# The second block's token mixers: spatial gating ahead of the context's output, a regrouped output projection, other PSUM banks, and the heads' transposes one unit later

## The chip, the cores and the metric

One core of a Trainium2 chip runs the whole program in one launch. The metric is device time in microseconds, lower is better; the profile's times are microseconds unless marked ns.

## The reference, cut to what matters

Two transformer blocks run one after the other on 512 tokens of width 1024. The change is in the second one, which has two layers and carries a context of 256 tokens beside x. In each layer the projected input is split into ten parts of 256 columns, and four mixers of 256 columns each are joined and projected:

```python
y_a = conformer_conv(a_val, a_gate, ...)      # 31-tap depthwise conv, layer norm, silu
y_b = diff_attention(q1, q2, k1, k2, v, ...)  # 4 heads, x attends to context and x; rms norm per head
y_c = spatial_gating(u, sv, ...)              # gelu, layer norm, a 128x128 token mix per chunk
y_d = short_conv_mixer(bg, cg, xin, ...)      # 3-tap depthwise conv between two gates
return concatenate([y_a, y_b, y_c, y_d], -1) @ w_out
```

Layer 0 runs these mixers for the context too (its attention sees only the context); layer 1 uses the context for keys and values alone. x then gets its gated sum and an MLP of width 4096.

## The kernel before, in words

Everything is in float32. A weight or activation that meets in a large matmul is split into a rounded part and a rest (`whalf`: `whi` on ACT at line 149, `wlo` on DVE at line 150; `split` for activations), and `mm3` makes three matmuls out of one (lines 157 to 159, `tok3` lines 164 to 166 where tokens are the stationary side). So one group of an input part is 2 halves x 4 k-tiles x 3 = 24 matmuls into one PSUM bank. Weights come by DMA into `raw` (4 buffers) and live in 3 buffers each of `whi` and `wlo`, for all stages.

The code is written with tiles and pools, and a planner makes each engine's stream from it ahead of time. It goes by program order, may bring forward what is ready, and a region under `bg()` or with a negative offset comes after work that stands later in the program. On the chip every engine runs its own stream in order. A tile waits for the tiles that had its place before; a pool takes the place of one that was closed.

The order of layer 0 of the second block, with its names: `mc` is the context's `Mixer`, `mx` that of x.

1. `mc.conv`, `mc.qkv`, `mc.spatial`, `mc.short`, then `mc.attention` in PSUM set `ps_k` (banks: g 4, mm 1, po 1, sc 2).
2. `mx.conv`, `mx.qkv` (parts 0, 1, 3, 4, 2 of x), still in `ps_k`.
3. `mc.conv_norm` (mean, square sums, rsqrt, silu of the convolution, lines 992 to 1013), then `mc.out_part("cdab")`: 8 output groups of 8 k-tiles, which write the context's sum back by DMA.
4. `mx.spatial`: part 6 by tokens, gelu and layer norm into `sv`; part 5, gelu; then 24 token-mix matmuls with `sv` into `ps.mm()` (lines 941 to 946), read by DVE at line 951.
5. `mx.attention` in set `ps_d` (g 3, mm 1, po 1, and three banks in one tile `sc3`). 16 units of one head and 128 queries: scores (line 1057), row maximum (DVE, line 1061), two exponentials (ACT, line 1065), the difference (DVE, line 1074), 6 transposes (line 1081), 12 matmuls with v (line 1084), which is 22 instructions of PE. `weights` of the next unit goes ahead of `apply` of this one. Each pair of heads ends in `heads_norm`, which scales the heads and transposes them (line 1106) into a y tile.
6. Work is hung into the units: at unit 1 `mx.short` (6 groups of 24 matmuls, under `bg()`), at unit 4 `mx.conv_norm`, then `out_part("cda")` under `bg()` (8 groups of 18), and one convolution tap of each half per unit while there are any left (line 872; the first 20 of 31 are given out earlier, under `bg(1000)`).
7. `out_part("b")` in set `ps_e` (8 groups of 6), each followed by the sum into x (line 1139) and its square, and the norm of x for the MLP.

Layer 1 has set `ps_m` (g 5, mm 3) for steps 2 and 4, the context's keys and values in step 2, and no step 1 and 3.

Of the kernel before, what the change touches and what calls it, by code (L numbers as in the profile page):

```python
# [19 lines left out]
P = 128  # L20
# [59 lines left out]
def tile_net(ctx: ExitStack, tc: tile.TileContext, wst, vec, crow, lrow, sgw, cst, xT, xN, cT, out):  # L80
# [14 lines left out]
    def close_pool(g):  # L95
        g.__exit__(None, None, None)
# [91 lines left out]
    def split(act, src, scale=None):  # L188

        if scale is None:  # L190
            A.copy(act[:, 0], src)
            V.tensor_sub(act[:, 1], src, act[:, 0].bitcast(F32))
        else:
            A.activation(act[:, 0], src, AF.Copy, scale=scale)
            V.scalar_tensor_tensor(act[:, 1], src, scale, act[:, 0].bitcast(F32), op0=ALU.mult, op1=ALU.subtract)
# [107 lines left out]
    ps = PS("ps_u", mm=8)  # L303
# [425 lines left out]
    def xsums():  # L729
        return Sums(SX, xp.tile([P, SX], F32, tag="acc", name=nm("acc")))  # L730
# [77 lines left out]
    class Mixer:  # L808
# [207 lines left out]
        def attention(self, k, bp, stp_, keys, between):  # L1016
# [9 lines left out]
            def load_head(h):  # L1026
                hd = Head()
                hd.h = h
                hd.q = stp_.tile([96, 2, s.n], F32R, tag="qst", name=nm("qst"), bufs=ST_BUFS)
                hd.k = stp_.tile([96, 2, nkeys], F32R, tag="kst", name=nm("kst"), bufs=ST_BUFS)  # L1030

                def stack(dst, src, blk, rows):
                    for i, hl in enumerate(rows):
                        nc.sync.dma_start(dst[32 * i:32 * i + 32].bitcast(F32),
                                          src[32 * blk:32 * blk + 32, hl].bitcast(F32))

                for w in range(2):
                    blk = 2 * (h % 2) + w
                    stack(hd.q[:, w], s.q[h // 2], blk, (0, 1, 0))
                    o = 0  # L1040
                    for q in keys:
                        stack(hd.k[:, w, o:o + q.n], q.k[h // 2], blk, (0, 0, 1))
                        o += q.n
                return hd
# [43 lines left out]
            def heads_norm(o, r1):  # L1088

                of = o.rearrange("p t h d -> p (t h) d")  # L1090
                rf = r1.rearrange("p t h -> p (t h)")
                sq = bp.tile([P, ng, 64], F32, tag="osq", name=nm("osq"), bufs=1)
                A.activation(sq, of, AF.Square)
                ms = const.tile([P, 16], F32, tag="ms", name=nm("ms"), bufs=3)
                m2 = const.tile([P, 16], F32, tag="ms2", name=nm("ms2"), bufs=2)
                V.tensor_reduce(ms[:, :ng], sq, axis=AX.X, op=ALU.add)
                V.tensor_mul(m2[:, :ng], rf, rf)
                V.tensor_mul(ms[:, :ng], ms[:, :ng], m2[:, :ng])
                V.tensor_scalar(ms[:, :ng], ms[:, :ng], 1.0 / 64.0, EPS, op0=ALU.mult, op1=ALU.add)
                rs = rstd_small(ms[:, :ng], ng)  # L1100
                V.tensor_mul(m2[:, :ng], rs[:, :ng], rf)
                V.tensor_mul(sq, of, m2[:, :ng].unsqueeze(2).broadcast_to([P, ng, 64]))
                pq = ps.mm()
                s2 = sq.rearrange("p (t h) d -> p t (h d)", h=2)
                for i in range(s.nt):
                    T.transpose(pq[:, i * P:(i + 1) * P], s2[:, i], ident)
                a = self.y_tile("b")
                split(a, pq[:, :s.n], k.subg)
                self.y["b", len([q for q in self.y if q[0] == "b"])] = a

            heads = {0: load_head(0)}
            units = [(h, qt) for h in range(4) for qt in range(s.nt)]
            nxt = weights(heads[0], 0)
            for un, (h, qt) in enumerate(units):
                hd = heads[h]
                if qt == 0:
                    if h < 3:
                        heads[h + 1] = load_head(h + 1)
                    if h % 2 == 0:
                        po = ps.mm("po")[:, :ng * 64].rearrange("p (t h d) -> p t h d", h=2, d=64)  # L1120
                        r1 = const.tile([P, s.nt, 2], F32, tag="r1", name=nm("r1"), bufs=2)
                    hd.r1 = r1
                    hd.po = po
                cur = nxt
                if un + 1 < len(units):
                    h2, qt2 = units[un + 1]
                    nxt = weights(heads[h2], qt2)
                apply(hd, qt, *cur)
                if un in between:
                    between[un]()  # L1130
                if self.taps[0] < 31:
                    self.conv_taps(k, self.taps[0] + CONV_STEP)
                if qt == s.nt - 1 and h % 2:
                    heads_norm(po, r1)


        def add(self, m, p, done):
# [5 lines left out]
        def out_part(self, names, done=None, bank=None):  # L1143
# [3 lines left out]
            for half in range(2):  # L1147
                w = {n: whalf((key, 2 + half), "ab".index(n), 512) for n in names if n in "ab"}
                for pair in range(2):
                    if "c" in names:  # L1150
                        w["cd"] = whalf((key, half), pair, 256)
                    for i in range(2):
# [9 lines left out]
                            mm3(p, hi[:, kk, c], lo[:, kk, c], a[:, 0], a[:, 1], e == 0, e == len(seq) - 1)  # L1162
                        self.add(4 * half + 2 * pair + i, p, done)


    g_ca, ctmp = open_pool("ctxb", side="right")
    kc = mix_consts(0, kvc, ctmp)
# [5 lines left out]
    mc.short()  # L1173
    close_pool(g_ca)
    ps.close()
    ps = PS("ps_k", g=4, mm=1, po=1, sc=2)
    g_cb, cb = open_pool("ctxb", side="right")
    mc.attention(kc, cb, cb, [sc], {})
    def load_rope(pool):
        rope = pool.tile([P, 2, SX], F32, tag="rope", name=nm("rope"))  # L1180
        nc.sync.dma_start(rope, cst[:, P + 9 * P:P + 9 * P + 1024].rearrange("p (a t) -> p a t", a=2))
# [7 lines left out]
    for l in range(2):  # L1189
# [2 lines left out]
        g_hc, hcp = open_pool("hc")  # L1192
        if l == 1:
            ps.close()
            ps = PS("ps_m", g=5, mm=3)
            kx = mix_consts(l, mix, hcp)
        else:
            kx = kc
# [7 lines left out]
            close_pool(g_c)  # L1206
        mx.qkv({"x": mix, "c": mix}, load_rope(hcp))
        close_pool(g_hc)
        if l == 0:

            mc.conv_norm(kc)
            sc.x = []
            for m in range(0, NT, 2):
                t = cmix.tile([P, 2, SC], F32R, tag="h", name=nm("xc"), bufs=8).bitcast(F32)
                nc.sync.dma_start(t, cT[:, m:m + 2])
                sc.x += [t[:, 0], t[:, 1]]
            mc.out_part("cdab", lambda m: nc.sync.dma_start(c_dram[m], sc.x[m]))
            close_pool(g_cb)
            close_pool(g_cm)
        g_st, stk = open_pool("stk")  # L1220
        g_y, yp = open_pool("yp", side="right")
        g_s, sgp = open_pool("sgp", side="right")
        mx.spatial(kx, sgp)
        close_pool(g_s)
        ps.close()
        ps = PS("ps_d", **PSD)
        g_b, bp = open_pool("mixb", side="right")
# [3 lines left out]
                mx.short()  # L1231

        def middle():
            mx.conv_norm(kx)
            with bg():
                mx.out_part("cda")

        mx.attention(kx, bp, stk, [sx, sc], {EARLY: early, MIDDLE: middle})
        close_pool(g_b)
        close_pool(g_st)  # L1240
        ps.close()
        ps = PS("ps_e", mm=8)
        sx.acc = xsums()
        mx.out_part("b", lambda m: sx.acc.add(None, sx.x[m], m, mx.tt("sq")))
        pbx = rstd_bcast(mix, sx.acc, SX, 1.0 / 1024, tile=mx.tt("rb"))
        close_pool(g_mix)
        close_pool(g_y)
        if l == 0:
            close_pool(g_kvc)

# [96 lines left out]
P_BUFS = 2  # L1347
HID_BUFS = 10
TA_BUFS = 6
CONV_TAPS = 20  # L1350
CONV_STEP = 1
CONV_BG = 1000
EARLY = 1
BIAS_BG = 200
MIDDLE = 4
ADA_HEAD = 0
PUMP = 6
L_BUFS = 8
# [146 lines left out]
```

## Time and profile before

| | us |
|---|---|
| median of 3 runs | 2176.56 (2175.21 to 2178.31) |
| the profiled execution | 2175.18 |
| its span, first to last instruction | 2173.3 |
| PE busy (matmuls) | 2053.4 |
| DVE busy | 1424.4 |
| ACT busy | 810.1 |
| layer 0, x's query projection to x's first scores | 787.3 to 860.7 |
| layer 0, x's attention, first scores to last product with v | 860.7 to 971.3 |
| layer 1, the same | 1661.6 to 1773.7 |

PE is TensorE's matmuls, PEld its weight loads, DVE VectorE, ACT ScalarE, POOL GpSimd, SP SyncE, which issues the DMAs. A busy share says how long an engine had something in hand, not that it was what the end waited for; matmuls are pipelined, so their number in a stretch says more than their busy time. A wait is told as: who waited, for whom, how long in all, how often, and the longest.

### The profile page before, as it was taken

Reading aid. Unit: us, or ns where it says so; the run is one execution under the profiler, and the core shown is the slowest. Engines: PE = TensorE matmul, PEld = TensorE weight load, DVE = VectorE, ACT = ScalarE, POOL = GpSimd, SP = SyncE. Lnnn points to the kernel's source line nnn. Section 1 sums busy time; section 2 is a strip of 40 time slices with the busy share of each in tenths; the row PEclk is TensorE's granted clock in tenths of the full one; section 3 lists DMA queues with packets and bytes.
Section 4 is the critical chain, followed back from the end, with each engine's and each line's share of the span. In section 5 each row is a group of like instructions: output and inputs, shape, how many; then the busy total and the mean of one; then the engine's idle time right before and its main releaser. Section 6 shows DMA issues by size and latency. Waiting matters only on the chain.

```text
span 2173.3 us, 28000 instructions
## 1 busy us (share of the span) xinstructions
PE 2053.4 (94%) x11020; PEld 1758.3 (81%) x11020; DVE 1424.4 (66%) x2351; ACT 810.1 (37%) x1266; POOL 27.4 (1%) x28
## 2 busy tenths in 40 slices
PE   7989999999999988998999999999998998999997
PEld 5778788778889777876888888888887787888886
DVE  8778999843458999778354645534798766443444
ACT  3565333432344533645312313123434544232331
POOL 0000000000000000000000000000000000000000
PEclk9999999999999999998999999999999998999998
DMA  8523666523335444222232454422413212333331
GB/s 314 171 92 95 197 222 204 181 94 105 109 111 168 124 121 127 78 78 79 67 127 88 138 169 150 155 67 89 135 59 107 83 59 69 97 97 97 97 97 58
DMA packets 84388, 259.47 MB, mean 119 GB/s; under 512 B 11424, under 2 KB 20256, under 8 KB 84256
## 3 DMA queue, kind: packets, MB, share of 16 engines
q1 hardware_dynamic: 84256, 257.67, 37.6%
q8 instruction: 87, 1.43, 0.3%
q14 instruction: 45, 0.37, 0.1%
HBM read 242.95 MB, written 5.24 MB: 114 GB/s over the span
## 4 chain that ended last, share of the span: by engine, by line
PE 72%; DVE 18%; DMA 3%; issue 3%; ACT 3%; POOL 1%; SPq 0%; POOLq 0%; DVEq 0%; ACTq 0%
PE mm L157 15%; PE mm L159 15%; PE mm L158 15%; PE g L157 5%; PE g L158 5%; PE g L159 5%; DVE wlo L150 3%; DVE ya L872 2%; PE po L1084 2%; DVE rawa L263 2%; DVE j L263 1%; PE sc L1057 1%; DMA rawa<-wst 1%; PE mm L1081 1%; PE mm L208 1%
## 5 line engine op out<-in xcount | busy, mean ns | idle before, releaser
L149 ACT CAST whi<-raw 128x1024 fp32r<-128x1024 f32 x312 | 326.9, 1050 | 536.7 <-PE mm L158 387.4
L150 DVE TENSOR_TENSOR wlo<-raw,whi 128x1024 fp32r<-128x1024 f32 x312 | 380.5, 1222 | 210.7 <-ACT whi L149 205.9
L157 PE MATMUL mm<-h,whi 128*128 128x512 f32 (+1 forms) x992 | 361.0, 366 | 5.7 <-ACT h L338 3.6
L158 PE MATMUL mm<-h,whi 128*128 128x512 f32 (+1 forms) x992 | 361.7, 365 | 0.9 <-DVE h L712 0.9
L159 PE MATMUL mm<-h,wlo 128*128 128x512 f32 (+1 forms) x992 | 361.1, 364 | 0.8 <-DVE wlo L150 0.8
L159 PE MATMUL mm<-hid,wlo 128*128 128x512 f32 (+1 forms) x768 | 272.6, 355 | 1.0 <-DVE wlo L150 1.0
L157 PE MATMUL mm<-hid,whi 128*128 128x512 f32 (+1 forms) x768 | 273.0, 355 | 0.0
L158 PE MATMUL mm<-hid,whi 128*128 128x512 f32 (+1 forms) x768 | 272.8, 355 | 0.0
L157 PEld LDWEIGHTS mm<-h,whi 128*128 128x128 f32 x992 | 188.8, 191 | 37.1 <-ACT h L338 4.0
L158 PEld LDWEIGHTS mm<-h,whi 128*128 128x128 f32 x992 | 188.7, 190 | 31.5 <-DVE h L712 1.9
L157 PE MATMUL g<-h,whi 128*128 128x512 f32 x512 | 205.7, 402 | 8.6 <-DVE v L508 6.0
L159 PEld LDWEIGHTS mm<-h,wlo 128*128 128x128 f32 x992 | 188.6, 190 | 31.2 <-DVE wlo L150 2.0
L158 PE MATMUL g<-h,whi 128*128 128x512 f32 x512 | 204.8, 400 | 0.0
L159 PE MATMUL g<-h,wlo 128*128 128x512 f32 x512 | 204.3, 399 | 0.3 <-DVE wlo L150 0.3
L159 PEld LDWEIGHTS mm<-hid,wlo 128*128 128x128 f32 x768 | 146.1, 190 | 21.5 <-DVE wlo L150 1.4
L157 PEld LDWEIGHTS mm<-hid,whi 128*128 128x128 f32 x768 | 146.4, 191 | 20.2
L158 PEld LDWEIGHTS mm<-hid,whi 128*128 128x128 f32 x768 | 146.3, 191 | 20.0
L1284 DVE SCALAR_TENSOR_TENSOR r<-mm,r 128x512 f32<-128x512 f32 x96 | 57.4, 599 | 114.1 <-ACT r L1283 114.0
L157 PEld LDWEIGHTS g<-h,whi 128*128 128x128 f32 x512 | 98.4, 192 | 26.9 <-issue 6.2
L159 PEld LDWEIGHTS g<-h,wlo 128*128 128x128 f32 x512 | 98.1, 192 | 19.3 <-DVE wlo L150 0.7
L158 PEld LDWEIGHTS g<-h,whi 128*128 128x128 f32 x512 | 98.3, 192 | 17.9
L872 DVE SCALAR_TENSOR_TENSOR ya<-glu,caw,ya 128x512 f32<-128x512 f32 (+1 forms) x180 | 111.6, 656 | 0.5
(309 smaller groups left out, 3462.7 us busy)
## 6 DMA issues: line engine op xcount, KB each, us to landing
raw<-wst SPq DMA_DIRECT2D x312, 512.0 KB, 3.9
rawa<-wst SPq DMA_DIRECT2D x120, 512.0 KB, 4.6
qst<-q SPq DMA_DIRECT2D x48, 64.0 KB, 2.0
kst<-k SPq DMA_DIRECT2D x48, 64.0 KB, 2.0
kst<-k SPq DMA_DIRECT2D x72, 32.0 KB, 2.1
x<-xT SPq DMA_DIRECT2D x4, 512.0 KB, 5.0
hs_d<-c SPq DMA_DIRECT2D x4, 512.0 KB, 2.6
hq<-hs_d SPq DMA_DIRECT2D x4, 512.0 KB, 5.5
```

What stands on the lines that cost most here:

```text
L149: A.copy(hi, src)
L150: V.tensor_sub(lo, src, hi.bitcast(F32))
L157: T.matmul(ps, lh, rh, start=start, stop=False)
L158: T.matmul(ps, lh, rl, start=False, stop=False)
L159: T.matmul(ps, ll, rh, start=False, stop=stop)
L208: T.matmul(pt[:, i:i + 1], a[:, i * P:(i + 1) * P], ones1, start=k == 0 and i == 0, stop=k == len(self.parts) - 1 and i == nt - 1, skip_gr ...
L263: V.tensor_tensor_reduce(o, w, row, 0.5, 0.0, ALU.mult, ALU.add, d)
L872: V.scalar_tensor_tensor(self.ya[m], x, w, self.ya[m], op0=ALU.mult, op1=ALU.add)
L1057: T.matmul(st[:, o:e], hd.q[:, w, qt * P:(qt + 1) * P], hd.k[:, w, o - w * nkeys:e - w * nkeys], start=True, stop=True, skip_group_check=True)
L1081: T.transpose(pt[:, i * P:(i + 1) * P], pw[0][:, t0 + i * P:t0 + (i + 1) * P], ident)
L1084: T.matmul(hd.po[:, qt, h % 2], pth[:, i * P:(i + 1) * P], ss.v[:, kt, h], start=i == 0 and qt == 0 and h % 2 == 0, stop=i == nk - 1 and q ...
L1284: V.scalar_tensor_tensor(r, p, 0.0, r, op0=ALU.max, op1=ALU.mult)
```

## The change

Five edits, in both layers where both have the place:

- The heads' end is cut in two. `heads_norm` scales the heads and returns `finish`, which transposes and splits them; `finish` of the first pair runs after the next unit's `apply`, that of the second pair is handed to the caller.
- x's `spatial` goes ahead of the context's `conv_norm` and `out_part`. For that the pool `yp` (x's y tiles) is opened before it and on the left side, and the context attention's pool `cb` is closed at once.
- x's output projection is grouped as c and d together, then a and b together (`out_ab`): the first three of its eight groups run their a and first b k-tiles ahead of `finish`.
- PSUM sets: `ps_k` has g 3 and mm 2 (before 4 and 1), `ps_m` g 3 and mm 2 (before 5 and 3); x's last projection stays in `ps_d`'s three g banks (before `ps_e`, eight).
- Hooks: 9 taps given out early (before 20), then 2 per unit (before 1); output c, d from unit 7; `conv_norm` at unit 11 (before 4, ahead of the output).

```diff
@@ -1100,14 +1100,19 @@
                 rs = rstd_small(ms[:, :ng], ng)
                 V.tensor_mul(m2[:, :ng], rs[:, :ng], rf)
                 V.tensor_mul(sq, of, m2[:, :ng].unsqueeze(2).broadcast_to([P, ng, 64]))
-                pq = ps.mm()
-                s2 = sq.rearrange("p (t h) d -> p t (h d)", h=2)
-                for i in range(s.nt):
-                    T.transpose(pq[:, i * P:(i + 1) * P], s2[:, i], ident)
-                a = self.y_tile("b")
-                split(a, pq[:, :s.n], k.subg)
-                self.y["b", len([q for q in self.y if q[0] == "b"])] = a
-
+
+                def finish():
+                    pq = ps.mm()
+                    s2 = sq.rearrange("p (t h) d -> p t (h d)", h=2)
+                    for i in range(s.nt):
+                        T.transpose(pq[:, i * P:(i + 1) * P], s2[:, i], ident)
+                    a = self.y_tile("b")
+                    split(a, pq[:, :s.n], k.subg)
+                    self.y["b", len([q for q in self.y if q[0] == "b"])] = a
+
+                return finish
+
+            pending = None
             heads = {0: load_head(0)}
             units = [(h, qt) for h in range(4) for qt in range(s.nt)]
             nxt = weights(heads[0], 0)
@@ -1126,12 +1131,16 @@
                     h2, qt2 = units[un + 1]
                     nxt = weights(heads[h2], qt2)
                 apply(hd, qt, *cur)
+                if pending:
+                    pending()
+                    pending = None
                 if un in between:
                     between[un]()
                 if self.taps[0] < 31:
                     self.conv_taps(k, self.taps[0] + CONV_STEP)
                 if qt == s.nt - 1 and h % 2:
-                    heads_norm(po, r1)
+                    pending = heads_norm(po, r1)
+            return pending
 
 
         def add(self, m, p, done):
@@ -1162,6 +1171,31 @@
                             mm3(p, hi[:, kk, c], lo[:, kk, c], a[:, 0], a[:, 1], e == 0, e == len(seq) - 1)
                         self.add(4 * half + 2 * pair + i, p, done)
 
+        def out_ab(self, done, finish):
+
+
+            key = f"out{self.l}"
+            ps_ = {}
+
+            def part(m, steps):
+                for e in steps:
+                    n, kk = "ab"[e // 2], e % 2
+                    (hi, lo), c, a = w[n], slice((m % 4) * P, (m % 4 + 1) * P), self.y["ab"[e // 2], kk]
+                    mm3(ps_[m], hi[:, kk, c], lo[:, kk, c], a[:, 0], a[:, 1], e == 0, e == 3)
+
+            for half in range(2):
+                w = {n: whalf((key, 2 + half), i, 512) for i, n in enumerate("ab")}
+                for m in range(4 * half, 4 * half + 4):
+                    if m == 0:
+                        for i in range(3):
+                            ps_[i] = ps.g()
+                            part(i, range(3))
+                        finish()
+                    if m > 2:
+                        ps_[m] = ps.g()
+                    part(m, range(3 if m < 3 else 0, 4))
+                    self.add(m, ps_[m], done)
+
 
     g_ca, ctmp = open_pool("ctxb", side="right")
     kc = mix_consts(0, kvc, ctmp)
@@ -1173,9 +1207,10 @@
     mc.short()
     close_pool(g_ca)
     ps.close()
-    ps = PS("ps_k", g=4, mm=1, po=1, sc=2)
+    ps = PS("ps_k", g=3, mm=2, po=1, sc=2)
     g_cb, cb = open_pool("ctxb", side="right")
-    mc.attention(kc, cb, cb, [sc], {})
+    mc.attention(kc, cb, cb, [sc], {})()
+    close_pool(g_cb)
     def load_rope(pool):
         rope = pool.tile([P, 2, SX], F32, tag="rope", name=nm("rope"))
         nc.sync.dma_start(rope, cst[:, P + 9 * P:P + 9 * P + 1024].rearrange("p (a t) -> p a t", a=2))
@@ -1192,7 +1227,7 @@
         g_hc, hcp = open_pool("hc")
         if l == 1:
             ps.close()
-            ps = PS("ps_m", g=5, mm=3)
+            ps = PS("ps_m", g=3, mm=2)
             kx = mix_consts(l, mix, hcp)
         else:
             kx = kc
@@ -1206,6 +1241,10 @@
             close_pool(g_c)
         mx.qkv({"x": mix, "c": mix}, load_rope(hcp))
         close_pool(g_hc)
+        g_y, yp = open_pool("yp")
+        g_s, sgp = open_pool("sgp", side="right")
+        mx.spatial(kx, sgp)
+        close_pool(g_s)
         if l == 0:
 
             mc.conv_norm(kc)
@@ -1215,13 +1254,8 @@
                 nc.sync.dma_start(t, cT[:, m:m + 2])
                 sc.x += [t[:, 0], t[:, 1]]
             mc.out_part("cdab", lambda m: nc.sync.dma_start(c_dram[m], sc.x[m]))
-            close_pool(g_cb)
             close_pool(g_cm)
         g_st, stk = open_pool("stk")
-        g_y, yp = open_pool("yp", side="right")
-        g_s, sgp = open_pool("sgp", side="right")
-        mx.spatial(kx, sgp)
-        close_pool(g_s)
         ps.close()
         ps = PS("ps_d", **PSD)
         g_b, bp = open_pool("mixb", side="right")
@@ -1231,20 +1265,19 @@
                 mx.short()
 
         def middle():
-            mx.conv_norm(kx)
             with bg():
-                mx.out_part("cda")
-
-        mx.attention(kx, bp, stk, [sx, sc], {EARLY: early, MIDDLE: middle})
+                mx.out_part("cd")
+
+        finish = mx.attention(kx, bp, stk, [sx, sc], {EARLY: early, MIDDLE: middle, LATE: lambda: mx.conv_norm(kx)})
+        sx.acc = xsums()
+        mx.out_ab(lambda m: sx.acc.add(None, sx.x[m], m, mx.tt("sq")), finish)
         close_pool(g_b)
         close_pool(g_st)
         ps.close()
         ps = PS("ps_e", mm=8)
-        sx.acc = xsums()
-        mx.out_part("b", lambda m: sx.acc.add(None, sx.x[m], m, mx.tt("sq")))
         pbx = rstd_bcast(mix, sx.acc, SX, 1.0 / 1024, tile=mx.tt("rb"))
+        close_pool(g_y)
         close_pool(g_mix)
-        close_pool(g_y)
         if l == 0:
             close_pool(g_kvc)
 
@@ -1347,12 +1380,13 @@
 P_BUFS = 2
 HID_BUFS = 10
 TA_BUFS = 6
-CONV_TAPS = 20
-CONV_STEP = 1
+CONV_TAPS = 9
+CONV_STEP = 2
 CONV_BG = 1000
+BIAS_BG = 200
 EARLY = 1
-BIAS_BG = 200
-MIDDLE = 4
+MIDDLE = 7
+LATE = 11
 ADA_HEAD = 0
 PUMP = 6
 L_BUFS = 8
```

## Rows read from the trace of the kernel before

**Rows 1.** The page: span, busy time of each engine, one DMA issue group (count, KB, us to landing).

```profile
span 2173.3 us, 28000 instructions
...
PE 2053.4 (94%) x11020; PEld 1758.3 (81%) x11020; DVE 1424.4 (66%) x2351; ACT 810.1 (37%) x1266; POOL 27.4 (1%) x28
...
kst<-k SPq DMA_DIRECT2D x72, 32.0 KB, 2.1
```

**Rows 2.** Stretches: length, busy us (instructions) of PE, PEld, DVE, ACT, POOL, granted clock, DMA.

```profile
660.00:670.00 10.00, 10.00 (x87) 9.99 (x86) 7.50 (x12) 4.92 (x9) 0.00 (x0) 1.00 0.61 200
...
776.70:787.30 10.60, 10.60 (x48) 8.77 (x48) 10.60 (x16) 3.24 (x5) 0.00 (x0) 1.00 0.32 99
787.30:860.70 73.40, 57.87 (x380) 53.12 (x379) 69.43 (x121) 23.91 (x33) 2.40 (x3) 0.91 0.45 135
...
860.70:870.00 9.30, 9.30 (x37) 7.41 (x36) 9.07 (x15) 3.12 (x7) 0.00 (x0) 0.79 0.52 169
870.00:910.00 40.00, 40.00 (x245) 34.23 (x244) 30.41 (x47) 24.66 (x49) 0.00 (x0) 1.00 0.32 89
860.70:971.30 110.60, 107.65 (x628) 90.47 (x628) 85.25 (x134) 62.39 (x121) 2.64 (x2) 0.98 0.26 77
...
1600.00:1650.00 50.00, 49.83 (x343) 46.17 (x341) 48.74 (x82) 17.52 (x27) 2.14 (x2) 1.00 0.34 98
1655.90:1661.60 5.70, 0.34 (x4) 0.17 (x3) 5.59 (x10) 1.46 (x3) 0.00 (x0) 0.86 0.25 59
1661.60:1670.00 8.40, 8.40 (x28) 6.81 (x29) 6.56 (x13) 2.49 (x5) 0.00 (x0) 0.69 0.61 186
```

**Rows 3.** Waits, 787.3 to 860.7, those of PE.

```profile
PE mm L157 <- DVE sb L951: 4.9, 3, 3.9
...
PE g L208 <- ACT sq L217: 4.3, 2, 3.3
...
PE g L241 <- DVE rb L238: 1.7, 1, 1.7
...
PE g L157 <- ACT whi L149: 1.5, 1, 1.5
PE g L159 <- DVE wlo L150: 1.5, 2, 0.9
```

**Rows 4.** Groups of PE, 787.3 to 860.7, shapes apart (count; busy, mean ns; idle before).

```profile
L157 PE MATMUL g<-y,whi 128*128 128x256 f32 x64 | 19.1, 306 | 2.3 <-ACT whi L149 1.5 <-ACT y L194 0.8
...
L164 PE MATMUL g<-whi,h 128*128 128x256 f32 x32 | 8.9, 283 | 0.0
...
L157 PE MATMUL mm<-sgs,sv 128*128 128x256 f32 x8 | 2.8, 351 | 4.9 <-DVE sb L951 4.9
```

**Rows 5.** Groups of DVE, 787.3 to 860.7, the convolution's taps of x.

```profile
L872 DVE SCALAR_TENSOR_TENSOR ya<-glu,caw,ya 128x512 f32<-128x512 f32 x47 | 33.1, 746 | 0.1
```

**Rows 6.** Waits of PE, layer 0's attention, 861 to 982.3.

```profile
PE mm L1106 <- DVE osq L1102: 3.7, 2, 2.1
```

**Rows 7.** Waits of PE, layer 1's attention, 1655.9 to 1784.8.

```profile
PE sc L1057 <- issue: 5.4, 1, 5.4
PE mm L1106 <- DVE osq L1102: 2.3, 2, 1.6
PE mm L1081 <- DVE y L195: 2.1, 1, 2.1
```

**Rows 8.** Timeline of DVE before layer 1's first scores (start, us).

```profile
1659.53 1.97 DVE L951 SCALAR_TENSOR_TENSOR sb<-mm,vecs,lrow 64x256 f32<-64x256 f32 x4
```

**Rows 9.** Groups of PE, 861 to 910.92: part of the short mixer's matmuls.

```profile
L157 PE MATMUL g<-h,whi 128*128 128x512 f32 x41 | 17.3, 421 | 0.0
```

**Rows 10.** Timeline of PE at `conv_norm`'s first matmuls, layer 0.

```profile
910.93 1.88 PE L997 MATMUL g<-ya,avg 128*128 128x512 f32 x4
```

**Rows 11.** Instructions on tile ya, 905 to 990 (min/median/max ns, first and last start).

```profile
L1010 DVE SCALAR_TENSOR_TENSOR ya<-th,ya x2: 686/686/686, 924.3 to 924.9; 128x512 f32<-128x512 f32 x2
...
L195 DVE SCALAR_TENSOR_TENSOR y<-ya,y x2: 685/686/686, 935.6 to 936.2; 128x512 fp32r<-128x512 f32 x2
```

## The prediction, made before the changed kernel ran

> **What bounds the kernel now.** First the page: PE is busy for 2053 of 2173 us [rows 1], so only stretches where it stands still, or runs slowly, can give time back; no edit here removes a matmul. Then the stretches [rows 2]. Layer 1's projections, 1600 to 1650, have 49.8 us of PE in 50: nothing to gain. Three others are thin. From x's query projection to its first scores in layer 0, 73.4 us, PE has 57.9 us and a granted clock of 0.91, a mean between 2.4 GHz and its lower level of 1.2; DVE is at 69.4. At the start of layer 0's attention the clock is 0.79, and PE does 37 instructions in 9.3 us where the steady stretch behind it does 245 in 40. In layer 1 the 5.7 us ahead of the first scores are empty, and the 8.4 us behind run at 0.69. Last the waits, for what ends them [rows 3, 6, 7].
>
> **x's spatial gating ahead of the context's output (layer 0).** The stretch of 73.4 us is a chain: the context's norm, with PE waiting 4.3 us for squares and 1.7 for the broadcast [rows 3]; the output, waiting 1.5 and 1.5 for whi and wlo; and x's gating, whose 24 token-mix matmuls wait 4.9 us for DVE to read the one mm bank. What must be issued: 3 x 64 output matmuls of 256 columns, 3 x 32 of part 6 and 3 x 8 of the token mix [rows 4], 312 in all, at 10/87 = 0.115 us: 35.9; and 48 of part 5 with 512 columns, which take 10.6 us in the query projection [rows 2]. With some 2 us of small matmuls that is 48.5 us, 24.9 less than now. The new order puts the gating where the norm's chain left PE empty, and the norm under part 5 and the gelus. What I expect to stay: the waits for weights, 1.5 + 1.5, since the output still keeps three of three `whi` buffers in use, and about 6 us of norm and gelu chain that overlap each other imperfectly while DVE is full (69.4 of 73.4). So 57.4 us, **-16.0**; bounds 0 and -24.9. With mm 2 instead of 1 the 4.9 us go; they are inside this sum.
>
> The x attention's loads move too: its pool now lies where the gating's tiles lay, so 18 loads of a head queue on SP behind the gating's end and not its start. They land in 2.1 us each [rows 1] and have the whole context output, over 22 us of PE, as cover; without it the first scores would wait for them. Queued behind them on SP are weight loads, which the 4 raw buffers cover. The context's write-back stays behind its sums; nothing of x waits for it.
>
> With the context's output last, x's scores, maxima and exponentials of the first units can run beside it. At the start of the attention PE now does in 9.3 us what takes 37 x 40/245 = 6.0: 3.3 us lost, of which I take **-2.0** (0 to -3.3).
>
> **Layer 1's start.** The three banks of `sc3` lie on those that the token mix used, and DVE reads the last of these until 1661.5 [rows 8]; the scores start there after 5.4 us [rows 7]. The new `ps_m` still puts mm under `sc3`, so that wait stays. But its five banks leave three for the short mixer's first groups, which before shared banks with the gating. Lost now: 5.7 us, and 8.4 - 28 x 40/245 = 3.8 in the slow stretch. I take **-3.5** of 9.5, near the lower third, since the weights of the short mixer pass the same full DVE.
>
> Fewer g banks (4 to 3, 5 to 3) I cost at nothing: in the attention stages three g banks already serve groups of 24, and PE's waits there name none for a bank [rows 6, 7]. Perfetto Trace Analysis in the Trainium skill says, under Optimizing Tensor Performance, that independent matmul groups should rotate through different PSUM banks, so that evacuation overlaps the next group; by that rule the change takes banks where they count, and the sum would be the rival's 2170 below in place of 2158. The waits with three banks do not show it.
>
> **Taps.** Taps fill DVE already: 47 of x's are in the stretch, 33.1 us [rows 5], though most are given out later in the program. New hooks change their rank, not their sum. I take nothing; the cover is DVE's idle time in the attention, 110.6 - 85.3 = 25.4 us [rows 2]. The rival on DVE prices its loss.
>
> **The heads' transposes.** PE waits for the scaled heads 3.7 us in layer 0 [rows 6], 2.3 in layer 1, and 2.1 there for the bank that holds the transposed heads [rows 7]: 8.1 us. One unit later, or behind 27 matmuls of the new projection (27 x 10.6/48 = 6.0 us), the chain is over in time: **-8.1** by itself. The context's two pairs are the same edit; a us at most, taken at nothing.
>
> **What takes its place: a comes late.** I read the g banks' order from this: in layer 0 `conv_norm` starts at 910.93 [rows 10], though the taps that it needs were over by then: 47 lie in the stretch before the attention [rows 5], none in it. Ahead of it are 41 + 40 + 40 = 121 matmuls of the short mixer (one of three rows is shown) [rows 9], that is five full groups of 24 and the first of the sixth. So a bank is given only after every group that the code asked for earlier has one, whatever its rank. In the new order the six groups and the eight of c and d stand ahead: 144 + 7 x 12 + 1 = 229 matmuls. Up to 910 PE has 37 + 245 = 282 instructions [rows 2], 121 of them filling; the other 161 are 7.3 units of 22. Some 25 of the filling lie in the slow start, so a unit takes (121 - 25)/7.3 = 13. Sixteen units take 208 to 216, and the start up to 25 more: `conv_norm` begins within a unit or two of the attention's end, and a comes after it. The projection a, b begins with a, so its 27 matmuls do not cover that. The chain took 924.9 + 0.7 - 910.9 = 14.7 us to its last multiply, and 25.3 us to the end of the split, which nobody hurried [rows 10, 11]; the split itself is two pairs of short instructions (0.69 on DVE). Without the attention's work beside it I take 13 us, between 10 and 25. Of these, PE has the last group's 12 matmuls (2.7 us) and the chain's own (3): idle 7 us in layer 0, and 5 in layer 1, where the start leaves more filling time. **+12**, and with the heads' -8.1, **+4** for both ends (bounds -8.1 and +32). No matmul is saved or added: 144 + 48 before, 96 + 96 now. The eight sums into x behind c, d and the eight behind a, b are 16 as before, and three banks in place of eight leave 2.7 us of PE's work to each sum on DVE.
>
> **Sum.** -16.0 - 2.0 - 3.5 + 4 = -17.5. From the profiled execution's 2175.2 (1.9 above its span, 1.4 below the median) that is 2157.7, forecast **2158 us**; its own range is 2150 to 2166.
>
> **The rivals.**
>
> *a is in time.* If filling goes faster than 13 a unit, or the norm is planned earlier, the ends give their whole 8.1: -16 - 2 - 3.5 - 8.1 = -29.6, 2146 us. For it: PE is denser than needed in the units. Against it: the place of the first average matmul [rows 9, 10].
>
> *DVE limits layer 0.* From 787.3 to 971.3 it has 69.4 + 85.3 = 154.7 us of work in 184.0, 84%. My sum wants 166 us for it, 93%, as full as the first part is now (95%), but for the whole length. At 89%, halfway, it takes 173.8: -10.2 in place of -18, so -9.7 in all, 2166 us. For it: the in-order waits on wlo. Against it: taps can wait until late in the attention.
>
> *Three banks are too few ahead of the attention.* Layer 1 has 17 groups there; if each waits for one DVE instruction of 0.69 [rows 11], 11.7 us come back: 2158 + 11.7 = 2170. Against it: the wait lists above.
>
> *Slower: a late, at full price.* If the chain takes its 25.3 us again after the attention, less 5.7 of PE's work, PE idles 19.6 us a layer, and the clock goes down as it did behind 5.7 empty us in layer 1. At 20 us each: -21.5 - 8.1 + 40 = +10.4, 2186 us. It decides from (21.5 + 8.1)/2 = 14.8 us a layer. For it: 25.3 us is measured. Against it: in that stretch the split was not next in line.
>
> *It does not do what it says.* PE's stream keeps the gating's tail and the output one behind the other, since buffers of `whi` bind: 2175 us. Against it: 3 us of waits for weights are all that the list has.
>
> **How the numbers follow.** Likeliest 0.45; a in time 0.15; DVE 0.15; banks 0.05; no effect 0.07; slower 0.13. 0.2% is 4.4 us, about what a measurement tells from no change. The first four are faster: 0.80; same 0.07; slower 0.13. A range from 2143 to 2178 leaves out most of the slower case and a tail of a in time, some 0.18.
>
> **What would show it.** Layer 0's stretch from the query projection to the first scores: some 57 us, with token-mix matmuls ahead of the context's output and no 4.9 us wait on sb. Waits on osq gone. `conv_norm`'s average within a unit of the attention's end and a PE wait for y of a few us there. Layer 1: short mixer's matmuls ahead of the scores. Wrong if the average comes earlier (then faster), if PE waits over 15 us for a (slower), or if the stretch stays above 65.

## The result: slower, and the profile after

The changed kernel takes 2190.48 us (median of 4, 2187.92 to 2192.18) beside 2175.89 for the kernel before in the same session: a ratio of 1.0065, interval 1.0047 to 1.0082. The forecast was 2158 and faster. The profiled execution took 2191.02 us. Its page, first the span and the busy row, then one DMA group:

```profile
span 2189.2 us, 28021 instructions
...
PE 2065.4 (94%) x11020; PEld 1764.6 (81%) x11020; DVE 1425.5 (65%) x2351; ACT 810.5 (37%) x1266; POOL 28.7 (1%) x28
...
kst<-k SPq DMA_DIRECT2D x72, 32.0 KB, 2.6
```

The work is the same: 11020 matmuls, 2351 instructions of DVE, as in [rows 1]. The profiled execution stands 5.3 us late already at x's query projection (792.6 against 787.3); 3.7 of that is there at 640 us, ahead of the first matmul that differs (at 727.9 in the kernel before). Up to that matmul the profiles of the other runs stand between 5.9 us earlier and 4.2 later with the same stream of PE, so stretches are compared, not times of day. The windows of layer 0 after, with the columns of [rows 2]: from the end of the query projection to the end of the context's output, then to x's first scores, to the first transposes, to the end of `conv_norm`'s first average (seven of c and d's eight groups are over by then), to the last product with v, to the norm's square sums:

```profile
792.60:859.30 66.70, 54.91 (x376) 50.15 (x375) 63.90 (x114) 23.74 (x34) 2.77 (x3) 0.95 0.37 117
859.30:872.50 13.20, 13.10 (x57) 10.52 (x58) 11.27 (x18) 3.86 (x5) 0.00 (x0) 1.00 0.60 168
872.50:893.00 20.50, 19.63 (x87) 15.67 (x86) 13.29 (x17) 7.28 (x13) 0.00 (x0) 1.00 0.56 157
893.00:937.00 44.00, 44.00 (x268) 37.14 (x267) 34.75 (x52) 25.49 (x52) 0.00 (x0) 1.00 0.40 108
937.00:987.50 50.50, 42.15 (x240) 35.86 (x238) 33.43 (x59) 26.39 (x55) 3.24 (x2) 0.81 0.11 34
987.50:1012.60 25.10, 19.73 (x77) 15.58 (x76) 16.26 (x28) 11.24 (x21) 1.64 (x1) 0.77 0.34 111
```

Two stretches changed. The first fell from 73.4 [rows 2] to 66.7 us. The attention with its end, 136.7 before (860.7 to 997.4), takes 153.3. (The very first score matmul before starts at 859.8; that moves 0.9 us from one of these stretches to the other, not their sum.) Layer 1, from one norm's square sums to the next, is 802.4 before and 802.8 after. That is +10.3 us of the 14.6.

The windows say what happened to the attention. Before its first transposes PE issues 57 + 87 = 144 matmuls in 33.7 us, nearly all of them the short mixer's; between 893 and 937 all is full. From 937 on little is left to fill with, 38 output matmuls; PE falls to 240 matmuls in 50.5 us, and the granted clock to 0.81 and 0.77. The longest waits of PE from 893 to 1012.6 are those of a bare chain (osq is the scaled heads, p the exponentials' difference, pth its transpose):

```profile
PE mm L1108 <- DVE osq L1102: 4.6, 1, 4.6
PE mm L1081 <- DVE p L1074: 2.9, 2, 2.6
PE sc L1057 <- ACT p L1065: 2.5, 2, 1.7
PE mm L1081 <- ACT pth L1082: 2.2, 3, 0.7
```

Why the units start late is seen on SP. First its row for these loads in the kernel before, then its timeline after, from the last of the context's write-back on (start, us, operation):

```profile
792.68 1.78 SPq L1034 DMA_DIRECT2D qst<-q  x3
```

```profile
853.56 5.95 SPq L1256 DMA_DIRECT2D c_dram<-xc  x3
860.99 0.33 SPq L140 DMA_DIRECT2D raw<-wst  x1
861.42 0.52 SPq L1034 DMA_DIRECT2D qst<-q  x1
862.79 2.13 SPq L140 DMA_DIRECT2D raw<-wst  x2
864.97 1.15 SPq L1034 DMA_DIRECT2D qst<-q  x2
866.16 1.86 SPq L1034 DMA_DIRECT2D kst<-k  x3
...
876.26 4.86 SPq L1034 DMA_DIRECT2D kst<-k  x6
```

The first load of head 0 goes out at 861.4, behind write-backs that wait for the output's last sums, and the last batch leaves from 876.3 on; in the kernel before these loads began at 792.7. The place that they are loaded into isn't what held them: the only work of another engine that the program lets the first one wait for is the gating's last token-mix matmul, which is over at 821.3. The output's last matmul starts at 858.4, so it covers none of them. The scores begin at 872.5, with one wait for a load. The last of the eighteen lands at 882.4, the first unit's last score follows at 884.8 and its first transposes, behind maximum and exponentials, at 893.0:

```profile
PE sc L1057 <- DMA kst<-k: 0.9, 1, 0.9
```

That row, of 859.3 to 893, is small because PE had the short mixer to do meanwhile. The lost time shows from 937 on, some 65 us later, when that filling is gone.

In layer 1 the wait ahead of the first scores is what it was [rows 7], and a new one stands before the projection of a, b. Its row names ms, but what that matmul reads is a, whose rounded half is over at the same time, 1788.8:

```profile
PE sc L1057 <- issue: 5.4, 1, 5.4
PE g L157 <- DVE ms L1098: 4.3, 1, 4.3
```

### The profile page after: what moved, and what is told of

It reads as the page before. It is cut to its first block, busy times and chain, and to the rows that moved or that the text cites. A ratio compares the mean times of both kernels' runs of the same rounds, so it can differ in the third digit from the quotient of the medians.

```text
span 2189.2 us, 28021 instructions
## 1 busy us (share of the span) xinstructions
PE 2065.4 (94%) x11020; PEld 1764.6 (81%) x11020; DVE 1425.5 (65%) x2351; ACT 810.5 (37%) x1266; POOL 28.7 (1%) x28
## 4 chain that ended last, share of the span: by engine, by line
PE 71%; DVE 16%; DMA 5%; issue 3%; ACT 3%; POOL 1%; SPq 0%; POOLq 0%; DVEq 0%; ACTq 0%
PE mm L157 15%; PE mm L159 15%; PE mm L158 15%; PE g L157 6%; PE g L158 5%; PE g L159 5%; DVE wlo L150 3%; DMA rawa<-wst 3%; DVE ya L872 2%; PE po L1084 2%; DVE rawa L263 2%; PE sc L1057 1%; DVE j L263 1%; POOL rs L225 1%; PE mm L1081 1%
## 5 line engine op out<-in xcount | busy, mean ns | idle before, releaser
L872 DVE SCALAR_TENSOR_TENSOR ya<-glu,caw,ya 128x512 f32<-128x512 f32 (+1 forms) x180 | 112.1, 656 | 0.5
```

Source lines behind the costliest of these rows:

```text
L872: V.scalar_tensor_tensor(self.ya[m], x, w, self.ya[m], op0=ALU.mult, op1=ALU.add)
```

## The experiments

All are kernels on the same chip as runs of the kernel before, which gave medians of 2174.4 to 2176.0. Theory A: the late loads of x's first head cost the time. Its rivals: B, a comes too late for the last projection; C, three banks are too few. Later runs take the other edits one by one, on top of the kernel with its loads early.

**The order undone.** The changed kernel with x's `spatial` behind the context's output again:

```diff
-        mx.spatial(kx, sgp)      # ahead of mc.conv_norm and mc.out_part
+        mx.spatial(kx, sgp)      # behind mc.out_part, as before
```

> The changed kernel with x's spatial gating behind the context's output again; all else as changed. Theory A (loads): the changed kernel loses because x's first q and k loads stand behind the context's write-back on SP's queue (861 us against 793 before), so that the short mixer's matmuls are used up ahead of the units and the second half of the attention is bare. With the gating behind the output, some 26 us of matmuls lie between the write-back and the scores: most of the 16.6 us that the attention and its end lost come back, and the 6.7 us that the first stretch gained are given up: about 2181 us. Theory B (a late): the end of the attention is slow because conv_norm stands behind eight output groups in the g banks; nothing changes there, and the first stretch loses its 6.7: about 2197 us. Theory C (banks): fewer g and mm banks are the loss: 2190 us, as changed.

2177.72 us, 1.0013 (1.0000 to 1.0026): the loss is gone, so it hangs on the order, and the other four edits together, with the old order, give no gain. The windows, from the first average matmul of the context to x's first scores and on to the first transposes:

```profile
787.40:852.90 65.50, 54.42 (x375) 49.96 (x375) 63.16 (x111) 22.52 (x31) 2.40 (x3) 0.95 0.48 143
852.90:868.90 16.00, 9.87 (x36) 7.41 (x35) 14.05 (x25) 3.99 (x9) 0.00 (x0) 0.86 0.45 133
```

With the old order the same stretch is as short (65.5) as with the new (66.7), so the gating's place by itself isn't what shortened it. A wait of the size of the one on sb [rows 3] returns behind the first scores, where PE stands for a g bank that a gelu reads (waits of PE, 852 to 1000):

```profile
PE g L157 <- DVE gu L913: 3.6, 1, 3.6
```

**The loads given out early.** The changed kernel, with head 0's loads of layer 0 ahead of the gating, in a pool of their own (`load_head` becomes a method; y tiles of b get a pool of their own):

```diff
+        if l == 0:
+            g_s0, st0 = open_pool("st0")
+            first = mx.load_head(0, st0, [sx, sc], 1)
         g_s, sgp = open_pool("sgp", side="right")
         mx.spatial(kx, sgp)
...
-            heads = {0: load_head(0)}
+            heads = {0: first or load_head(0)}
```

> The changed kernel with head 0's q and k loads of x in layer 0 given out ahead of the spatial gating, into a pool of their own. Theory A (loads): first scores right behind the context's output, near 860 us and not 872 to 889, the short mixer's matmuls spread over the units, 10 to 14 us back: 2176 to 2180 us. Theory B (a late) and theory C (banks): 2190 us, within 3.

2166.62 us, 0.9956 (0.9940 to 0.9973): 23.9 us less than the changed kernel, more than the 10 to 14 that theory A gave, and faster than the kernel before. SP's timeline has q's loads at 792.3 to 796.8, and k's before them:

```profile
771.74 2.40 SPq L1024 DMA_DIRECT2D kst<-k  x4
...
792.31 0.51 SPq L1024 DMA_DIRECT2D qst<-q  x1
793.18 0.33 SPq L140 DMA_DIRECT2D raw<-wst  x1
793.78 3.06 SPq L1024 DMA_DIRECT2D qst<-q  x5
```

The windows that answer to those above, the first scores now at 859.2, right behind the output:

```profile
790.50:859.10 68.60, 58.06 (x376) 53.47 (x375) 63.31 (x112) 22.80 (x33) 2.77 (x3) 0.88 0.39 119
859.10:871.00 11.90, 11.60 (x54) 9.08 (x52) 11.76 (x17) 5.87 (x12) 0.00 (x0) 1.00 0.61 164
871.00:917.00 46.00, 46.00 (x283) 39.11 (x282) 37.93 (x62) 28.29 (x56) 0.00 (x0) 1.00 0.40 106
917.00:966.80 49.80, 47.78 (x289) 39.55 (x289) 40.32 (x67) 28.21 (x55) 2.64 (x2) 1.00 0.21 66
```

The last 50 us of the attention hold 289 matmuls where the changed kernel has 240, at a clock of 1.00 instead of 0.81. The attention with its end is 133.8 us, 19.5 less; the first stretch is no shorter (68.6). The late loads are the cause of the loss.

**The convolution's norm earlier.** LATE 11 to 6, so that a is not behind c and d's output; once on the changed kernel, once with the loads early.

```diff
-LATE = 11
+LATE = 6
```

> The changed kernel with conv_norm at unit 6, so that it asks for its g banks ahead of the eight output groups of c and d (unit 7). Theory B (a late): conv_norm starts after the sixth short group, a is there long before the attention ends in both layers, the 4.7 us wait in layer 1 and several us in layer 0 go: 2180 to 2184 us. Theory A (loads): only layer 1's wait goes, layer 0's attention still runs out of filling matmuls: 2185 to 2187 us. Theory C (banks): 2190 us.

> Early loads of x's head 0 as in the run before, and conv_norm at unit 6, ahead of the output groups of c and d. If a late costs what it seems to there (conv_norm's first matmul at 954 of an attention that ends at 967, then waits of some 3 us in layer 0 and 5 in layer 1): 2159 to 2163 us. If what the late a costs is given back by filling that is used up sooner (as far as conv_norm at unit 6 alone gave only 2.7 us without the early loads): 2164 to 2167 us.

2187.78 us (1.0051, 1.0033 to 1.0069) and 2166.19 (0.9955, 0.9938 to 0.9971). A late a costs about 2.7 us of the changed kernel, which the two intervals do not tell from nothing, and nothing that can be measured once the loads are early. The average moves from 954.3 to 907.8 there, but the attention is longer (square sums at 997.4 against 992.9, from the same first scores). That c and d are missing as filling would explain it, but this profiled execution also took 6.3 us more than the median, so it is not shown.

**The banks undone.**

```diff
-    ps = PS("ps_k", g=3, mm=2, po=1, sc=2)
+    ps = PS("ps_k", g=4, mm=1, po=1, sc=2)
-            ps = PS("ps_m", g=3, mm=2)
+            ps = PS("ps_m", g=5, mm=3)
```

> The changed kernel with the banks of before: ps_k with g 4 and mm 1, ps_m with g 5 and mm 3. Theory C (banks): 5 us or more come back, under 2186 us. Theories A (loads) and B (a late): the ends stay as they are; one mm bank puts up to 5 us of token-mix waits into layer 0: 2190 to 2195 us.

2191.88 us, 1.0068 (1.0047 to 1.0088): no effect on the time. It also says more of the first stretch: with the new order and the old banks that takes 66.6 us (783.1 to 849.7), and PE waits 2.2 us there for sb, 0.8 with two mm banks and 4.9 in the kernel before. So the new order and the second mm bank each shorten that wait, and the stretch is no shorter with both than with one (65.5, 66.6 and 66.7).

**The context's norm ahead of the gating** (loads early), to see whether its chain can hide:

```diff
+        if l == 0:
+            mc.conv_norm(kc)
         mx.spatial(kx, sgp)
-            mc.conv_norm(kc)
```

> Early loads of x's head 0, and the context's conv_norm ahead of x's spatial gating, with the context's output still behind it. If the first stretch shrank by 6.7 us only because the context's norm asks for its g banks behind the gating's four groups, and so runs bare after them, its waits (1.5 + 2.7 + 2.1 us) go under the gating's matmuls: 2158 to 2162 us. If DVE limits that stretch (74.6 of 80 us busy), the order does not matter: 2165 to 2168 us.

2186.74 us, 1.0039 (1.0024 to 1.0054), a miss for every theory. The stretch is hardly shorter, 67.4 us: the norm's chain stays bare wherever it stands, and the waits of PE up to 855 say so.

```profile
PE g L208 <- ACT sq L217: 4.4, 2, 3.4
...
PE g L241 <- DVE rb L238: 1.7, 1, 1.7
```

In the profile 18 of the 20 us came later, from the first scores (852.4) to the square sums: 152.1 us for 133.8. The waits, from 855 on:

```profile
PE g L157 <- ACT y L194: 5.1, 2, 4.3
PE mm L1081 <- DVE p L1074: 3.6, 1, 3.6
PE sc L1057 <- ACT p L1065: 3.2, 1, 3.2
```

The tap runs below show the same three waits without this edit, so this run doesn't price it.

**The output's grouping and the hooks undone** (loads early): c, d, a as before, b in `ps_e`, `conv_norm` at unit 4.

```diff
-                mx.out_part("cd")
+                mx.out_part("cda")
...
-        mx.out_ab(lambda m: sx.acc.add(None, sx.x[m], m, mx.tt("sq")), finish)
+        finish()
+        mx.out_part("b", lambda m: sx.acc.add(None, sx.x[m], m, mx.tt("sq")))
```

> Early loads of x's head 0, but x's output projection grouped as before (c, d, a in the attention, b behind it in eight banks, conv_norm at unit 4, the second pair's transposes ahead of it). If the new grouping gains at the very end, where the first matmul of the square sums follows the last output matmul after 0.2 us and not 4.0, and loses less by the late a: 2170 to 2174 us. If the late a costs as much or more: 2160 to 2167 us.

2168.76 us, 0.9958 (0.9943 to 0.9974), between the two sizes expected and the same as with the new grouping within the noise. With groups of 6 the sums into x lag, and the norm of x waits for acc (waits of PE, 850 to 990):

```profile
PE mm L208 <- DVE acc L221: 4.2, 1, 4.2
```

With groups of 12 that is gone (the square sums follow 0.2 us after the last matmul begins, 4.0 before). Against it stand a wait of 1.5 us for the last square behind them and, in layer 1 alone, the late a: 4.3 + 0.8 us that the old grouping does not have.

**The first pair's transposes at once** (loads early):

```diff
+                    if h == 1:
+                        pending()
+                        pending = None
```

> Early loads of x's head 0, and the first pair's transposes at once, as before, instead of one unit later. If the deferral saves the waits for osq that the profile of before shows for the first pairs (2 us in layer 0, 1 in layer 1, and 2 for the bank behind): 2170 to 2172 us. If the next pair's products with v wait for the same chain through their one bank: 2165 to 2168 us.

2174.1 us (2167.88 to 2177.81), 0.9991 (0.9977 to 1.0005): taking the first pair's delay back costs 7.5 us, give or take some 5. Its waits of PE in the two attentions, layer 0's row first; with the delay, what is left of the pair is a wait for the po bank, 0.4 and 1.0 us:

```profile
PE mm L1108 <- DVE osq L1102: 1.5, 2, 1.1
...
PE mm L1108 <- DVE osq L1102: 3.1, 2, 2.2
```

**The taps** (loads early): 20 given out early and 1 per unit, as before, then 4 and 3.

```diff
-CONV_TAPS, CONV_STEP = 9, 2
+CONV_TAPS, CONV_STEP = 20, 1     # the other run: 4, 3
```

> The kernel of e2_loads (2166.6 us) with the taps as before: 20 given out early, then one per unit. Theory: the taps' rank is worth nothing, since DVE has idle time in the attention; 2164 to 2170. Rival (DVE limits layer 0): with 20 taps early, more of x's taps stand ahead of the gating's gelus and the first stretch grows, or with 9 early they crowd the attention; then 3 us or more either way.

> The kernel of e2_loads with 4 taps given out early and 3 per unit (9 and 2 there, 20 and 1 in e12_taps). Theory: what the taps cost is the place of the first units' maxima and of the weights' rests in DVE's stream ahead of and behind the first scores; each tap taken from there brings PE's filling matmuls forward, so fewer early taps give the same 2166.6 or up to 4 us less, 2162 to 2167. Rival (the stretch ahead is not what counts, only that the taps end by unit 11): 2166 to 2168. Against both: three taps of two halves per unit, 4.4 us of DVE in a unit of about 6.5, crowd the units themselves, 2170 and more.

2178.32 us (1.0016, 1.0005 to 1.0028) and 2178.81 (1.0016, 1.0006 to 1.0027). Both cost 12 us, so both theories missed; the first run's rival had 3 or more, and "crowd the units", which fits the second time, is not seen: the attention up to its last product is 105.5 us there, 107.9 with 9 taps. The number of taps is not why, since it goes both ways. What the two share in the traces is DVE's order at the first scores. First the kernel with 9 taps, then the one with 4:

```profile
860.45 1.22 DVE L150 TENSOR_TENSOR wlo<-raw,whi 128x1024 fp32r<-128x1024 f32 x1
861.59 1.75 DVE L1061 TENSOR_REDUCE sm<-sc 128x2 f32<-128x1536 f32 x1
863.26 0.74 DVE L872 SCALAR_TENSOR_TENSOR ya<-glu,caw,ya 128x512 f32<-128x512 f32 x1
863.92 1.22 DVE L150 TENSOR_TENSOR wlo<-raw,whi 128x1024 fp32r<-128x1024 f32 x1
```

```profile
856.33 1.75 DVE L1061 TENSOR_REDUCE sm<-sc 128x2 f32<-128x1536 f32 x1
858.00 1.41 DVE L872 SCALAR_TENSOR_TENSOR ya<-glu,caw,ya 128x512 f32<-128x512 f32 x2
...
865.24 1.20 DVE L150 TENSOR_TENSOR wlo<-raw,whi 128x1024 fp32r<-128x1024 f32 x1
```

With 9 taps the rests of the short mixer's weights stand among the first maxima, and PE does 42 of its matmuls before the first transposes. With 4 (and with 20) the next rest comes at 865; PE does 6, then stands for its second scores and first transposes. Its waits from 785 to 1015 with 4 taps; with 20 these three rows are the same:

```profile
PE g L157 <- ACT y L194: 5.9, 3, 4.3
...
PE mm L1081 <- DVE p L1074: 3.6, 1, 3.6
...
PE sc L1057 <- ACT p L1065: 3.2, 1, 3.2
```

So less filling is done early, and c and d's groups come later: 69 of their 96 matmuls start before the last product with v, with 9 taps all of them. `conv_norm` begins at 963.8, after that product (959.7; with 9 taps 954.3 and 966.8), and the projection waits for a 5.1 us (0.8 of the row's 5.9 stand in the context's output). The stretch from the last product to the square sums takes 43.3 us instead of 25.8. That is the forecast's "a late" in layer 0, triggered from the other end of the stage. No run changes DVE's order alone, so that the order is the cause is read from the traces, not shown.

**Layer 1's banks turned round**: the tag that a set is first asked for gets its first banks, so with this line the score tile lies on g banks and not on the token mix's. Alone, and with the old grouping (loads early in both):

```diff
-            pr = ps.mm()
+            pr = ps.g() if l else ps.mm()
```

> The kernel of e2_loads with the PSUM set of layer 1's projections laid out the other way round: its g banks come first and lie under the three score banks, its mm banks under po and the transposes. Theory: layer 1's first scores wait 5.6 us because the token mix's last bank lies under the score tile; with it elsewhere the scores start as soon as their q and k are there, the wait is under 2 us, and the time falls by 2 to 5 us, to about 2162. Rival (the wait is for something else that ends at the same time, a load of head 0 or the clock): no change, 2166.

> The kernel of e10_group (loads early, output grouped as before, 2168.8 us) with the same turned PSUM set in layer 1. If the 5.6 us wait is the bank's, it gives the same 2 to 5 us as in e14_order1: 2164 to 2167. If grouping c with d pays only once layer 1's start is dense, e14_order1 is ahead of this one by more than 3 us.

2167.23 us (0.9957, 0.9942 to 0.9972) and 2172.22 (0.9979, 0.9966 to 0.9993): no gain, so the rival's number. The wait ahead of the scores shrinks from 5.3 to 3.2 us, now for a gelu that reads a g bank, and a rest of the weights is waited for as well (waits of PE, 1640 to 1800, of the first run). In both profiles layer 1 is 6 us longer than without the edit (806.9 and 806.3 against 800.8 and 800.3); the medians show 0.6 and 3.5 of that.

```profile
PE g L159 <- DVE wlo L150: 3.6, 1, 3.6
PE sc L1057 <- DVE gu L913: 3.2, 1, 3.2
```

## Why the prediction was wrong

**The step that failed** is that of the moved loads: "They land in 2.1 us each [rows 1] and have the whole context output, over 22 us of PE, as cover". The landing was right enough (2.6 us in the median of these loads), the cover wrong. The text put the loads behind the gating on SP and looked only at what is queued behind them. The context's write-back, which it named two sentences later ("nothing of x waits for it"), was ahead of them in the same in-order queue, and its last transfers wait for the output's last sums. So the first load went out after the stage that was to hide it. The text gave the consequence ("without it the first scores would wait") and no price; measured, it is 23.9 us. No rival had it: "Slower: a late, at full price" came within 5 us of the result by another mechanism, so by luck.

The sum, term by term, as measured in stretches of layer 0 and as the span from norm to norm for layer 1:

| step | forecast | changed kernel | with the loads early |
|---|---|---|---|
| layer 0, first stretch | -16.0 | -6.7 | -4.8 |
| layer 0, attention's start and end | -2 + 2 | +16.6 | -2.9 |
| layer 1 | -3.5 + 2 | +0.4 | -1.6 |
| sum | -17.5 | +10.3 | -9.3 |

With the loads mended the sum of stretches, -9.3, agrees with the ratio's -9.6; the rest of the changed kernel's +14 lies ahead of these stretches, within the scatter between profiles (the query projection stands at 787.3 before, at 792.6 in the changed kernel and at 790.5 with the loads early), and is not explained further.

**The first stretch** was mis-sized by more than half, and stayed above the 65 us that the prediction itself had named as a sign of being wrong. It is 9.3 us over the forecast 57.4. Of these 6.4 are PE's own work: 48.5 were costed, from rows at a clock of 1.00, and PE is busy for 54.9 at a granted clock of 0.95 (58.1 at 0.88 with the loads early). The other 2.9 are waits: 11.8 us idle where 3 + 6 were kept. "The new order puts the gating where the norm's chain left PE empty" did not happen: the waits on squares and rb are 4.0 and 1.7 us after, 4.3 and 1.7 in [rows 3]. The bank order that the prediction itself had read put the norm's groups behind the gating's (the context's first average stands at 817.8, 787.5 before). Asking for them first didn't help, so the banks are not the whole of it. DVE is busy for 63 to 64 us of 65.5 to 68.6 in the stretches shown, which is what the rival "DVE limits" would have, in this stretch and not in the whole layer. But some 27 us of that are 38 or 39 taps of x that nothing waits for before `conv_norm`, and no run took work from DVE there, so whether DVE sets this length stays open.

**Layer 1's start**, -3.5 forecast, gave next to nothing: from the norm's square sums to the first scores 663.3 us for 664.2. The wait stayed as foretold, and free banks did not bring the short mixer forward: 4 of its matmuls stand in the 8 us ahead of the scores, as before. With the banks turned round there are 10, and then PE waits 3.6 us for a rest that DVE has to make, as the prediction had feared ("the same full DVE"). The layer's ends come to +1.3 for +2: the attention takes 105.8 us for 112.1, its end 33.7 for 26.1.

**The ends.** The reading of the banks' order was right: in the changed kernel the average stands at 934.6, at the 85th matmul of c and d (7 x 12 + 1). In layer 1 a is late and costs 4.3 + 0.8 us of waits, as much as the 5 forecast; in layer 0 it is all but in time, in the changed kernel (0.8 us) and with the loads early (1.1). The heads' -8.1 was of the right order: about 7.5 for the first pair alone; the second pair's part was not measured by itself, and in the changed kernel one wait on osq of 4.6 us is left. The chain's 25.3 us "to the end of the split" in the prediction reach to the start of the split's last instruction, 26.0 to its end; no term changes by more than that. The sum into x, costed as no change, gave back 3.8 us a layer (4.0 to 0.2), less 1.5 for the last square.

**At nothing** were the banks (right: 2191.88 against 2190.48) and the taps. The taps' work does hide, but changing their rank costs 12 us with the loads early. The Trainium skill's rule of rotating PSUM banks (Perfetto Trace Analysis, Optimizing Tensor Performance), which spoke against this change, is not seen to bind here: with four and five banks in place of three the time is the same, 2191.88 against 2190.48 us.

## What to carry to other kernels

When a step is moved, list for each transfer what is ahead of it in its in-order queue and what those wait for, not only what queues behind it; a write-back behind a sum ends its stage, and a load behind that write-back has no cover. Filling hides a late start only until it runs out: look for the loss where the filling should have been, tens of microseconds later. And before a gap is counted as gain, cost PE's work at the clock that the stretch is granted, and see which engine's work would have to fit into the gap; here the stretch became as short without moving the gating.

## What the runs showed that was not expected

- The same edit of one constant to either side (4, 9 and 20 taps) gave 2178.8, 2166.6 and 2178.3 us. A planner's order switches between two forms at the first scores, and three kernels (both tap runs and the context's norm) show the same waits of 3.2 and 3.6 us there. What makes it switch stays open.
- A wait in the list can be a twentieth of its cost: 0.9 us for the load in layer 0, 19.5 us in the stage's length. Part of that is the clock, which was granted at 0.81 and 0.77 of full speed in the two stretches where PE had gaps, and at 1.00 where it had none.
